# Windowed attention with a sink: the masks move from TensorE products into VectorE's maximum

## The chip, the cores and the metric

The kernel runs on one core of a Trainium2 chip. The metric is the device time of one execution in microseconds (us); a kernel's figure is the median of its timed runs. The core's engines are named as in the profile: PE is TensorE (PEld its weight loads), DVE is VectorE, ACT is ScalarE, POOL is GpSimd and SP is SyncE, which issues most DMAs.

## The reference, cut to what matters

The model is two layers deep, 512 tokens and 256 context tokens wide, with a width of 1024. The first layer ("even") has a gated chunk mixer and a differential attention, the second ("odd") the attention of this change. Each layer ends in a feed-forward of width 2816. The odd attention has 16 query heads of 64 over 4 key heads. A block of 128 queries sees the block before, its own and the next one (within a distance of 128), and all 256 context keys. A learned sink per head enters the softmax as one more score without a value.

```python
mask = ((kpos >= 0)[None, :] & (kpos < s_len)[None, :]
        & (jnp.abs(qpos[:, None] - kpos[None, :]) <= WINDOW))
return sink_attend(qb, [(kb, vb, mask), (kc, vc, None)], sink)
...
def sink_attend(q, kvs, sink):
    ...
        s = jnp.einsum('bqhgd,bkhd->bhgqk', q, k).astype(jnp.float32) * ATTN_SCALE
        if mask is not None:
            s = jnp.where(mask, s, NEG_INF)
    ...
    p = jax.nn.softmax(jnp.concatenate(scores + [s_sink], axis=-1), axis=-1)
```

## The kernel before, in words

Everything is held transposed on chip, features on the 128 partitions, and dense products are made of three products of split operands (a rounded high part and a low part, `mm3`, lines 111 to 117). The stages follow each other: even mixer, feed-forward 0, odd mixer, feed-forward 1. Within a stage the Tile framework's scheduler (`schedule_with_timeline_sim=True`, line 2037) puts the instructions into each engine's queue in an order that it works out from its own timeline; `tc.issue_after` and the helper `run` (lines 46 to 50) tie some of them to a fixed order. Each engine then runs its queue strictly in order. A tile with `bufs=n` has n buffers in turn, and a writer waits until the readers of the old content are done.

Ahead of the odd attention, the keys and values of both kinds of tokens are projected and the keys are rotated and split (`stack`, lines 1740 to 1746). In that stretch the mask is prepared: a DMA brings 128 x 384 values (0 or -1e30) into `mraw`, ScalarE copies its first and last 128 columns into `mask`, copies the identity into `identr`, copies the sink to `sink` and negates `nsink` (lines 1709 to 1715), and takes one exponential so that its table is loaded (line 1716).

`odd` (line 1766) runs `attend(g, half)` for the four key heads g with half 0, then with half 1; each half has two blocks i of 128 queries, so there are 16 row blocks, and `softmax` makes four score tiles (one per query head of the group) in each: 64 tiles. For one tile PE makes the products with the two key parts into a PSUM tile `pw` (lines 1801 to 1803); adds the mask to each neighbour block by a product of the identity and the mask (lines 1804 to 1808); and makes the context products (lines 1809 to 1811). Blocks 0 and 3 have 512 scores a row and one masked neighbour, blocks 1 and 2 have 640 and two, so there are 96 mask products. PSUM tiles of scores come from `wide`, which has two buffers; a buffer holds two tiles of 512 or one of 640.

VectorE then finds the negative row maximum (line 1814) and takes the minimum with the negated sink (line 1815). ScalarE reads the scores from PSUM, adds that value, takes the exponential into the SBUF buffer `e` (7 buffers) and sums the row (line 1817). Four small operations give the reciprocal of the row's sum with the sink (lines 1819 to 1822). PE transposes the exponentials (lines 1839 to 1841), VectorE and ScalarE in turn copy them from PSUM into `pt` (line 1843), and PE multiplies them with the values (lines 1848 to 1853).

PE's other work in this stretch is the projection of later query heads (`project_q`), the output projection of the first half (`project(0, ...)`, line 1911) and the start of that of the second half (lines 1916 to 1927).

Of the kernel before, what the change touches and what calls it, by code (L numbers as in the profile page):

```python
# [7 lines left out]
F32R = mybir.dt.float32r  # L8
BF16 = mybir.dt.bfloat16
I32 = mybir.dt.int32  # L10
AF = mybir.ActivationFunctionType
ALU = mybir.AluOpType
AX = mybir.AxisListType.X

P = 128
# [3 lines left out]
TC = 256  # L19
# [8 lines left out]
class Builder:  # L28
# [17 lines left out]
    def run(self, key, fn, *args, **kw):  # L46

        with self.tc.issue_after(self.tail[key].ins) if key in self.tail else ExitStack():
            self.tail[key] = fn(*args, **kw)  # L49
        return self.tail[key]  # L50
# [1478 lines left out]
    def seam(self, s2_part, Wl, ahead):  # L1529

        tc, nc, a, run = self.tc, self.nc, self.a, self.run
# [5 lines left out]
        X, C = [[[t[:, c] for t in A] for A in self.A] for c in (slice(0, TX), slice(TX, TA))]  # L1537
# [86 lines left out]
        ps = self.fill()  # L1624
# [52 lines left out]
        def products(upto):  # L1677
            for v in order:
                if v == "s":
                    csum.append(self.single())  # L1680
                    sums(csum[0], [sq[1, m] for m in (0, 3, 4, 5, 6, 7)], TC)
                elif v == "d":
                    csum.append(spread(csum[1], self.single()))
                else:
                    (k_x if v[0] == "K" else v_x)(int(v[1]))
                if v == upto:
                    return
# [18 lines left out]
                self.ring, self.ring_cfg = wide  # L1706
        csum.append(diagonal(csum[0], TC))
        products("V7")
        mask = Rk.tile([P, 2, P], F32R, name="mask")
        identr = Rk.tile([P, P], F32R, name="identr")  # L1710
        sink = Rk.tile([P, 16], F32, name="sink2")
        run("ACT", nc.scalar.copy, mask, mraw.rearrange("p (a c) -> p a c", a=3)[:, 0::2, :])
        run("ACT", nc.scalar.copy, identr, self.ident)
        run("ACT", nc.scalar.copy, sink, nsink)
        run("ACT", nc.scalar.mul, nsink, nsink, -1.0)
        run("ACT", nc.scalar.activation, self.small(16), nsink, AF.Exp)
# [3 lines left out]
        qps = [self.fill(), self.single()]  # L1720
        for ps, W2 in zip(qps, Wq):
            for k in range(KT):
                t, c = W2[k // 4], k % 4 * P
# [3 lines left out]
        b = self.bank()  # L1727
# [8 lines left out]
        K = []  # L1736
# [17 lines left out]
        V = []  # L1754
        for tb in range(6):
            v = Rk.tile([P, TC], F32, name=f"v1_{tb}")
# [4 lines left out]
        self.ring, self.ring_cfg = kept  # L1761
        Rt.release()
        self.here = here
        self.kv = qps, X, Rk, tabs, K[0] + K[1], V, mask, identr, sink, nsink

    def odd(self):
        tc, nc, a = self.tc, self.nc, self.a
        qps, X, Rk, tabs, K, V, mask, identr, sink, nsink = self.kv
        Rs = tc.alloc_tile_pool(name="att1", bufs=1, side="right", reuse_waits="tile")
        Qs, scored = {}, {}  # L1770
        stacks = [Rk.tile([P, TX], F32R, name=self.uid(t), tag="sq01", bufs=4) for _ in range(2) for t in ("qa", "qb")]
# [11 lines left out]
        def softmax(g, i, rc):  # L1783


            nm, sums, sk = [self.small(4, "sa", 10) for _ in range(3)]
            b0, b1 = max(0, i - 1), min(4, i + 2)
            w = (b1 - b0) * P
            edge = w + TC <= TX
            st = 0 if edge else TX - w  # L1790
            en = st + w
            es = []
            for x in range(4):
                pair, par = x // 2, x % 2
                if edge:
                    two = self.wide() if par == 0 else two
                    ps = two[:, par * TX:par * TX + TX]
                else:
                    ps = self.wide()
                Q = Qs[2 * g + pair][par][:, i * P:(i + 1) * P]  # L1800
                for p in range(2):
                    nc.tensor.matmul(ps[:, st:en], Q, K[g][p][:, b0 * P:b1 * P], start=p == 0, stop=p == 1,  # L1802
                                     skip_group_check=True)
                for b in range(b0, b1):
                    if b != i:
                        c = st + (b - b0) * P
                        nc.tensor.matmul(ps[:, c:c + P], identr, mask[:, int(b > i), :], start=False, stop=True,
                                         skip_group_check=True)
                for p in range(2):
                    last = nc.tensor.matmul(ps[:, en:en + TC], Q, K[g][p][:, TX:], start=p == 0 and not edge,  # L1810
                                            stop=p == 1, skip_group_check=True)
                scored[g, i, x] = last
                c = nm[:, x:x + 1]
                nc.vector.tensor_reduce(c, ps[:, st:en + TC], axis=AX, op=ALU.max, negate=True)
                nc.vector.tensor_tensor(c, c, nsink[:, 4 * g + x:4 * g + x + 1], ALU.min)
                e = Rs.tile([P, 640], F32, name=self.uid("e"), tag="e1", bufs=7)
                nc.scalar.activation(e[:, :w + TC], ps[:, st:en + TC], AF.Exp, bias=c, accum_out=sums[:, x:x + 1])
                es.append(e)
            nc.vector.tensor_tensor(sk, nm, sink[:, 4 * g:4 * g + 4], ALU.add)
            nc.scalar.activation(sk, sk, AF.Exp)  # L1820
            nc.vector.tensor_tensor(sums, sums, sk, ALU.add)
            nc.vector.reciprocal(rc, sums)
            return es, b0, b1
# [92 lines left out]
        for m in range(2):  # L1916
# [4 lines left out]
            ps = both[:, m * TC:(m + 1) * TC]  # L1921
# [119 lines left out]
```

## Time and profile before

| | |
|---|---|
| median of 3 runs | 1554.86 us (1551.56 to 1555.87) |
| profiled execution | 1551.89 us, span 1550.1 us |
| PE, PEld busy | 1496.6 us (97%), 1344.5 us (87%) |
| DVE, ACT, POOL busy | 1080.4 us (70%), 736.4 us (48%), 816.4 us (53%) |
| granted TensorE clock, mean | 0.997 |

The profile is of one execution. A row of a group names the line of the kernel, the engine, the operation, the tiles it writes and reads, shape and count; then the busy time of the group in us, the mean of one in ns, and the idle time of the engine just before, with what ended it. A row of the timeline begins with start and duration in us; in brackets stands the idle time before it and who ended it. Matmuls are pipelined, so their durations overlap and the distance of starts tells what one costs. "issue" is idle time without a visible cause. A wait for several things is put down to the last of them.

### The profile page before, as it was taken

How to read it: one execution, taken by the hardware profiler on the slowest of the kernel's cores; microseconds unless marked ns; L12 is line 12 of the kernel's file. 1: busy time of each engine (PE TensorE's matmuls, PEld its weight loads, DVE VectorE, ACT ScalarE, POOL GpSimd, SP SyncE). 2: the span in 40 equal slices, each digit the busy share in tenths (PEclk: the TensorE clock that was granted, in tenths of full speed). 3: DMA queues.
4: the chain of work that ended last, by engine and by line, in shares of the span. 5: the costliest groups of instructions: out<-in, count | busy, mean ns of one | idle time of the engine just before them, and what ended most of it. 6: DMA issues, size and time to landing. Idle time of an engine off the chain costs nothing.

```text
span 1550.1 us, 25119 instructions
## 1 busy us (share of the span) xinstructions
PE 1496.6 (97%) x9611; PEld 1344.5 (87%) x9611; DVE 1080.4 (70%) x1922; ACT 736.4 (48%) x1515; POOL 816.4 (53%) x556
## 2 busy tenths in 40 slices
PE   6999899899999999999999998999989999999998
PEld 5758789799989999999999887777869899999997
DVE  6622888765887877888885577665667966666665
ACT  4525566554543333333333345556556544444444
POOL 1353320053077677668776535432314488888882
PEclk9999999999999999999999999999999999999999
DMA  9881100251043243445441312100224232323201
GB/s 352 297 296 51 38 8 1 65 208 41 28 130 116 96 130 116 134 159 170 139 167 52 102 43 68 48 28 21 69 96 164 66 112 90 115 89 116 89 21 55
DMA packets 55464, 162.27 MB, mean 105 GB/s; under 512 B 6192, under 2 KB 8624, under 8 KB 47664
## 3 DMA queue, kind: packets, MB, share of 16 engines
q1 hardware_dynamic: 48288, 135.37, 26.0%
q10 hardware_dynamic: 7056, 25.30, 4.9%
q8 instruction: 75, 1.23, 0.3%
q14 instruction: 45, 0.37, 0.1%
HBM read 158.55 MB, written 2.10 MB: 104 GB/s over the span
## 4 chain that ended last, share of the span: by engine, by line
PE 82%; DVE 13%; ACT 3%; issue 2%; DMA 0%; POOL 0%; DVEq 0%; SPq 0%; ACTq 0%; POOLq 0%
PE pw L116 11%; PE pw L115 11%; PE pw L117 11%; PE pb L115 8%; PE pb L116 8%; PE pb L117 8%; PE pf L115 4%; PE pf L116 4%; PE pf L117 4%; PE pb L1851 2%; PE pb L1840 2%; PE pw L1802 1%; PE pw L1810 1%; PE pf L369 1%; DVE t L49 1%
## 5 line engine op out<-in xcount | busy, mean ns | idle before, releaser
L999 DVE SCALAR_TENSOR_TENSOR xT<-pb,mod,xT 128x512 f32<-128x512 f32 (+3 forms) x204 | 143.2, 709 | 128.7 <-PE pb L117 128.3
L115 PE MATMUL pw<-ax,w 128*128 128x384 f32 (+2 forms) x716 | 226.5, 318 | 3.7 <-DVE q L49 1.9
L116 PE MATMUL pw<-ax,w 128*128 128x384 f32 (+2 forms) x716 | 227.4, 318 | 2.6 <-DVE ax L49 2.4
L117 PE MATMUL pw<-ax,w 128*128 128x384 f32 (+2 forms) x716 | 226.9, 317 | 0.1
L49 POOL TENSOR_TENSOR w<-raw,w 128x512 fp32r<-128x512 f32 x122 | 186.0, 1540 | 48.2 <-ACT w L49 48.1
L92 POOL TENSOR_TENSOR w<-raw,w 128x512 fp32r<-128x512 f32 (+1 forms) x70 | 103.2, 1482 | 161.6 <-ACT w L89 151.4
L49 POOL TENSOR_TENSOR w<-t,w 128x512 fp32r<-128x512 f32 x99 | 147.9, 1498 | 56.3 <-ACT w L49 56.3
L115 PE MATMUL pb<-hh,w 128*128 128x512 f32 x480 | 171.2, 357 | 2.2 <-DVE xT L999 2.2
L117 PE MATMUL pb<-hh,w 128*128 128x512 f32 x480 | 171.7, 358 | 0.4 <-DVE w L49 0.4
L116 PE MATMUL pb<-hh,w 128*128 128x512 f32 x480 | 171.3, 357 | 0.0
L115 PE MATMUL pw<-T,w 128*128 128x384 f32 (+1 forms) x508 | 156.6, 310 | 2.5 <-DVE hs L1207 1.2
L116 PE MATMUL pw<-T,w 128*128 128x384 f32 (+1 forms) x508 | 157.0, 310 | 1.2 <-DVE T L132 1.2
L117 PE MATMUL pw<-T,w 128*128 128x384 f32 (+1 forms) x508 | 157.0, 310 | 0.0
L115 PE MATMUL pf<-ax,w 128*128 128x256 f32 (+2 forms) x460 | 150.5, 327 | 2.9 <-DVE qf L264 1.1
L117 PE MATMUL pf<-ax,w 128*128 128x256 f32 (+2 forms) x460 | 149.5, 325 | 0.0
L116 PE MATMUL pf<-ax,w 128*128 128x256 f32 (+2 forms) x460 | 148.8, 323 | 0.0
L115 PEld LDWEIGHTS pw<-ax,w 128*128 128x128 f32 x716 | 135.5, 190 | 8.5 <-DVE q L49 2.6
L116 PEld LDWEIGHTS pw<-ax,w 128*128 128x128 f32 x716 | 136.0, 190 | 7.8 <-DVE ax L49 3.6
L117 PEld LDWEIGHTS pw<-ax,w 128*128 128x128 f32 x716 | 136.0, 190 | 2.4 <-DVE w L1170 0.4
L49 POOL TENSOR_TENSOR hh<-hs,hh 128x768 fp32r<-128x768 f32 (+1 forms) x42 | 78.0, 1858 | 92.9 <-ACT hh L49 69.1
L49 POOL TENSOR_TENSOR w<-rawo,w 128x512 fp32r<-128x512 f32 x59 | 103.8, 1760 | 29.5 <-ACT w L49 29.5
L240 DVE SCALAR_TENSOR_TENSOR junk<-ar,cb 128x1024 bf16<-128x1024 f32 x64 | 106.8, 1669 | 0.0
(442 smaller groups left out, 3912.0 us busy)
## 6 DMA issues: line engine op xcount, KB each, us to landing
raw<-ffn_in SPq DMA_DIRECT2D x44, 1024.0 KB, 5.3
ar<-ada SPq DMA_DIRECT2D x24, 1024.0 KB, 7.9
ar<-ada ACTq DMA_DIRECT2D x48, 512.0 KB, 3.6
rawo<-ffn_out SPq DMA_DIRECT2D x88, 256.0 KB, 3.0
raw<-odd_out SPq DMA_DIRECT2D x28, 256.0 KB, 2.7
raw<-qk SPq DMA_DIRECT2D x16, 256.0 KB, 7.8
raw<-uv SPq DMA_DIRECT2D x16, 256.0 KB, 3.2
raw<-even_out SPq DMA_DIRECT2D x8, 512.0 KB, 3.5
```

Of the source, the lines that this page charges most:

```text
L49: self.tail[key] = fn(*args, **kw)
L92: eng.tensor_tensor(lo, raw, hi.bitcast(F32), ALU.subtract)
L115: mm(out, s[0], m[0], start=start, stop=False, **kw)
L116: mm(out, s[0], m[1], start=False, stop=False, **kw)
L117: return mm(out, s[1], m[0], start=False, stop=stop, **kw)
L240: return self.nc.vector.scalar_tensor_tensor(junk, t, 1.0, self.cb[who], ALU.mult, ALU.mult, accum_out=self.acc[who][:, col:col + 1])
L369: return run("PE", fn, *args, **kw) if head else fn(*args, **kw)
L999: ins = self.nc.vector.scalar_tensor_tensor(h, ps[:, r], self.modcol(l, j, m, who), h, ALU.mult, ALU.add)
L1802: nc.tensor.matmul(ps[:, st:en], Q, K[g][p][:, b0 * P:b1 * P], start=p == 0, stop=p == 1, skip_group_check=True)
L1810: last = nc.tensor.matmul(ps[:, en:en + TC], Q, K[g][p][:, TX:], start=p == 0 and not edge, stop=p == 1, skip_group_check=True)
L1840: last = nc.tensor.transpose(pt[:, x * P:(x + 1) * P], es[2 * (x % 2) + x // 2][:, kb * P:(kb + 1) * P], self.ident)
L1851: nc.tensor.matmul(po[64 * h:64 * h + 64, :], V[vb][:, 64 * g:64 * g + 64], t[:, h * TC:h * TC + TC], start=kb == 0, stop=kb == nb - 1, sk ...
```

## The change

`mask` becomes a row of six blocks of 128 in bf16: lower neighbour, own, upper neighbour, and three of zeros; GpSimd clears it and ScalarE writes the two neighbour blocks. `identr` and the mask products go. One VectorE instruction per tile adds the tile's stretch of `mask` to the scores, multiplies by -1, writes the result into `e`, and takes the minimum over the row with the negated sink as its first value. The exponential then reads `e` in SBUF, with scale -1 and that minimum as its bias, and writes it in place. Block 3, which has its lower neighbour and own block ahead of the context, reads the row of six in two runs of 256.

```diff
-        mask = Rk.tile([P, 2, P], F32R, name="mask")
-        identr = Rk.tile([P, P], F32R, name="identr")
+        mask = Rk.tile([P, 6, P], BF16, name="mask")
+        nc.gpsimd.memset(mask, 0.0)
         sink = Rk.tile([P, 16], F32, name="sink2")
-        run("ACT", nc.scalar.copy, mask, mraw.rearrange("p (a c) -> p a c", a=3)[:, 0::2, :])
-        run("ACT", nc.scalar.copy, identr, self.ident)
+        run("ACT", nc.scalar.copy, mask[:, 0:3:2, :], mraw.rearrange("p (a c) -> p a c", a=3)[:, 0::2, :])
...
-                for b in range(b0, b1):
-                    if b != i:
-                        c = st + (b - b0) * P
-                        nc.tensor.matmul(ps[:, c:c + P], identr, mask[:, int(b > i), :], start=False, stop=True,
-                                         skip_group_check=True)
                 for p in range(2):
                     last = nc.tensor.matmul(ps[:, en:en + TC], Q, K[g][p][:, TX:], start=p == 0 and not edge,
                                             stop=p == 1, skip_group_check=True)
                 scored[g, i, x] = last
                 c = nm[:, x:x + 1]
-                nc.vector.tensor_reduce(c, ps[:, st:en + TC], axis=AX, op=ALU.max, negate=True)
-                nc.vector.tensor_tensor(c, c, nsink[:, 4 * g + x:4 * g + x + 1], ALU.min)
                 e = Rs.tile([P, 640], F32, name=self.uid("e"), tag="e1", bufs=7)
-                nc.scalar.activation(e[:, :w + TC], ps[:, st:en + TC], AF.Exp, bias=c, accum_out=sums[:, x:x + 1])
+                s, t = ps[:, st:en + TC], e[:, :w + TC]
+                if i == 3:
+                    cut = lambda v: v.rearrange("p (a c) -> p a c", a=2)
+                    s, u, m = cut(s), cut(t), cut(mask.rearrange("p b c -> p (b c)"))[:, :, :TC]
+                else:
+                    u, m = t, mask.rearrange("p b c -> p (b c)")[:, (i == 0) * P:(i == 0) * P + w + TC]
+                nc.vector.tensor_tensor_reduce(u, s, m, -1.0, nsink[:, 4 * g + x:4 * g + x + 1], ALU.add, ALU.min, c)
+                nc.scalar.activation(t, t, AF.Exp, bias=c, scale=-1.0, accum_out=sums[:, x:x + 1])
                 es.append(e)
```

More of the change, by code (lines that the diff above doesn't have):

```diff
@@ L1763, in seam @@
         self.here = here
-        self.kv = qps, X, Rk, tabs, K[0] + K[1], V, mask, identr, sink, nsink
+        self.kv = qps, X, Rk, tabs, K[0] + K[1], V, mask, sink, nsink
     def odd(self):
         tc, nc, a = self.tc, self.nc, self.a
-        qps, X, Rk, tabs, K, V, mask, identr, sink, nsink = self.kv
+        qps, X, Rk, tabs, K, V, mask, sink, nsink = self.kv
         Rs = tc.alloc_tile_pool(name="att1", bufs=1, side="right", reuse_waits="tile")
```

## The prediction, made before the changed kernel was timed

> **What bounds the kernel now.** I read the page first, for the shares of the engines and the chain.
>
> ```profile
> span 1550.1 us, 25119 instructions
> ...
> PE 1496.6 (97%) x9611; PEld 1344.5 (87%) x9611; DVE 1080.4 (70%) x1922; ACT 736.4 (48%) x1515; POOL 816.4 (53%) x556
> ...
> PE 82%; DVE 13%; ACT 3%; issue 2%; DMA 0%; POOL 0%; DVEq 0%; SPq 0%; ACTq 0%; POOLq 0%
> ```
>
> TensorE (PE) is busy nearly all the time and holds 82% of the chain that ended last. That is an average, so the next view is the table of stretches. The first score product of the odd attention starts at 959.83 us and its last transposes end near 1156.8 us; what follows is the projection's end and the second feed-forward.
>
> ```profile
> 959.83:1156.80 196.97, 189.26 (x1322) 147.40 (x1321) 124.20 (x289) 112.59 (x270) 61.44 (x56) 0.99 0.16 53
> 963.00:970.00 7.00, 4.80 (x18) 3.94 (x19) 4.28 (x11) 3.87 (x9) 5.05 (x4) 0.76 0.24 75
> 1157.00:1551.00 394.00, 379.84 (x2679) 355.04 (x2677) 263.93 (x433) 195.12 (x414) 283.95 (x193) 0.99 0.28 91
> ```
>
> The columns after the stretch are its length, then busy time of PE, PEld, DVE, ACT and POOL, then the granted clock and the DMAs. In the 197.0 us of the attention PE lacks only 7.7 us of being always busy. VectorE (DVE) has 72.8 us free and ScalarE (ACT) 84.4. So work taken from PE should show in the time, and VectorE has room for more. After 1157 us PE is busy for 379.84 of 394.00 us and starts from the attention's result, so that part should simply begin earlier by what the attention saves. The waits of PE in the attention say the same:
>
> ```profile
> PE pw L1802 <- ACT e L1817: 3.1, 1, 3.1
> PE pb L1840 <- ACT e L1817: 2.5, 4, 1.5
> PE pf L115 <- DVE qf L264: 1.1, 1, 1.1
> ```
>
> One wait of 3.1 us is for a score bank that ScalarE still reads, and four waits of 2.5 us together are for exponentials to transpose.
>
> **The change, part by part. Mask products.** What one costs can't be read from its duration, since matmuls overlap; it is read from starts.
>
> ```profile
> L1807 PE MATMUL pw<-mask,identr x96: 219/223/307, 960.3 to 1148.4; 128*128 128x128 f32 x96
> ```
> ```profile
> 1023.30 0.28 PE L1802 MATMUL pw<-kl,qb 128*128 128x256 f32 x1
> ...
> 1023.42 0.22 PE L1807 MATMUL pw<-mask,identr 128*128 128x128 f32 x1
> ...
> 1023.48 0.33 PE L1810 MATMUL pw<-kh,qb 128*128 128x256 f32 x1
> ...
> 1023.65 0.28 PE L1810 MATMUL pw<-kl,qb 128*128 128x256 f32 x1
> ...
> 1023.77 0.28 PE L115 MATMUL pf<-ax,w 128*128 128x256 f32 x1
> ```
>
> From the mask's start to that of the second context product are 0.23 us, in which one mask product and one 256-column product run. The 256-column products beside them follow each other at 0.12 us. So a mask costs about 0.115 us: 0.06 for itself and the rest because the next product waits for its weights. 96 of them are 11.0 us, all on PE.
>
> **VectorE: two operations become one.** Now each of the 64 score tiles has a maximum and a small minimum.
>
> ```profile
> L1814 DVE TENSOR_REDUCE sa<-pw 128x1 f32<-128x640 f32 x32 | 26.1, 821 | 5.9 <-PE pw L1810 5.4
> ...
> L1814 DVE TENSOR_REDUCE sa<-pw 128x1 f32<-128x512 f32 x32 | 21.7, 686 | 16.7 <-PE pw L1810 16.4
> L1815 DVE TENSOR_TENSOR sa<-sa,sink 128x1 f32<-128x1 f32 x64 | 15.0, 240 | 1.0
> ```
>
> That is 26.1 + 21.7 + 15.0 = 62.8 us, 0.98 us a tile. The fused operation does not occur in this trace. The nearest rows read a PSUM bank and an SBUF tile and write SBUF; one more prices the reading of an accumulator.
>
> ```profile
> L999 DVE SCALAR_TENSOR_TENSOR xT<-pb,mod,xT 128x512 f32<-128x512 f32 x175 | 129.9, 747 | 122.2 <-PE pb L117 121.9
> ...
> L999 DVE SCALAR_TENSOR_TENSOR xT<-pb,mod,xT 128x256 f32<-128x256 f32 x22 | 10.2, 480 | 2.9 <-PE pb L117 2.9
> ...
> L240 DVE DVE_READ_ACCUMULATOR junk<-ar,cb 128x1 f32 x64 | 5.1, 79 | 0.0
> ```
>
> 256 elements more cost 747 - 480 = 267 ns, so 640 elements are an estimated 747 + 133 = 880 ns. The low end is one pass with nothing more, 32 x (0.747 + 0.880) = 52.1 us; with a separate accumulator read of 79 ns it is 57.2 us. The high end is two passes, the elementwise row plus the reduction's: 0.747 + 0.686 = 1.43 us and 0.880 + 0.821 = 1.70 us, together 100.4 us. I take one pass and the read, 57.2 us: the row of line 999 has the same two kinds of operands and does its arithmetic in one pass. VectorE is then 5.6 us less busy, off PE's path, and worth nothing by itself. The fourth row block's mask is read in two runs of 256; I cost that at zero, since the element count stays 512, and up to some tens of ns could hide in VectorE's free time.
>
> **ScalarE reads SBUF in place of PSUM.**
>
> ```profile
> L89 ACT CAST w<-raw 128x512 fp32r<-128x512 f32 x72 | 44.2, 620 | 55.3 <-PE pw L117 30.0 <-PE pf L117 13.6 <-DMA raw<-odd_out 4.2
> ...
> L1843 ACT COPY pt<-pb 128x512 f32<-128x512 f32 x40 | 23.4, 586 | 19.7 <-PE pb L1840 19.6
> ```
>
> A cast from SBUF takes 620 ns where a copy from PSUM takes 586, so the exponential becomes about 34 ns longer, 2.2 us over 64, beside 84 us that ScalarE has free. It reaches PE only where PE waits for an exponential: at most once in each of 16 row blocks, 0.5 us. [...]
>
> **Banks come free earlier.** Now a score bank is held until the exponential has read it; after the change until VectorE has. Its worth is read from the one long wait, at the start:
>
> ```profile
> 959.42 3.51 DVE L1746 TENSOR_TENSOR kl<-kf,kh 64x256 fp32r<-64x256 f32 x8
> ...
> 962.85 1.28 DVE L1814 TENSOR_REDUCE sa<-pw 128x1 f32<-128x512 f32 x2
> ...
> 964.37 0.69 ACT L1817 ACTIVATE e<-pw,sa 128x512 f32<-128x512 f32 x1 [0.87 <-DVE sa L1815]
> ...
> 965.20 0.38 PE L1802 MATMUL pw<-kh,qb 128*128 128x256 f32 x1 [3.11 <-ACT e L1817]
> ```
>
> VectorE is held by the key split until 962.85, whatever PE does. The first fused operation then ends at 962.85 + 0.75 = 963.60, and PE follows 0.14 us later (as now, 964.37 + 0.69 to 965.20), at 963.74: 1.46 us earlier. The two masks ahead of this wait (0.23 us) save nothing, since the wait swallows them.
>
> **The e buffer is taken earlier.** The fused operation writes e, so it must wait until the transposes of the row block before have read the buffer (7 buffers, 4 tiles a block: the fourth tile reuses the first of the block before). The old maximum did not wait for that. Behind it in VectorE's queue stand copies of transposed tiles (L1843), the row sums and the rope of the next queries; PE's value products wait for those copies. The closest case in the trace is:
>
> ```profile
> 1028.23 0.60 PE L1840 MATMUL pb<-ident,e 128*128 128x128 f32 x4
> ...
> 1028.50 0.69 DVE L1814 TENSOR_REDUCE sa<-pw 128x1 f32<-128x512 f32 x1 [0.79 <-PE pw L1810]
> ```
>
> The transposes end at 1028.83, so the fused operation would start 0.33 us late, and VectorE had idled 0.79 us before anyway. I take zero; the high end is a rival below.
>
> **Setup.** A POOL memset of 768 elements a partition, a cast of the identity less, and ScalarE's mask cast now waits for the memset.
>
> ```profile
> L744 POOL MEMSET kl<- 64x768 f32 x2 | 1.5, 734 | 0.1
> ```
> ```profile
> 928.91 1.29 POOL L265 TENSOR_TENSOR sh<-sh,sin 128x512 f32<-128x512 f32 x1 [6.87 <-DVE sh L263]
> ```
> ```profile
> 929.94 0.37 ACT L1757 COPY v<-pb 128x256 f32<-128x256 f32 x1 [6.88 <-PE pb L117]
> ```
>
> The memset takes some 0.73 us behind the weight splits, and 6.87 us of POOL's idle time follow before the rope. Behind ScalarE's wait stand the small sink operations and the table load, and then 6.88 us of idle time. Cost zero; without that cover, 0.7 us.
>
> **The sum.** 94 masks that the first wait does not swallow are 94 x 0.115 = 10.8 us; the bank wait 1.46; together 12.3. Against it: where PE waits for an exponential, up to one mask a block (16 x 0.115 = 1.8 us) is swallowed in the same way; I take half, 0.9. The longer exponential, 0.5 at most: 0.4. That leaves 11.0 us. The profiled execution took 1551.89 us (1550.1 of span and 1.8 around it), so 1540.9 for one like it. The runs lie between 1551.56 and 1555.87, with the median 1554.86, 3.0 above the profiled one; against the median it is 1543.9.
>
> **The rivals.** *A larger gain, through the clock.* After the first wait the granted clock was 0.76 over 963 to 970, which is 7 x 0.24 = 1.7 us lost; a wait at 1239 did the same.
>
> ```profile
> 1239.32 0.38 PE L115 MATMUL pw<-ax,w 128*128 128x256 f32 x1 [1.90 <-DVE q L49]
> ```
> ```profile
> 1239.60:1243.00 3.40, 3.40 (x15) 3.18 (x15) 3.40 (x5) 0.12 (x1) 3.40 (x3) 0.51 0.21 63
> ```
>
> If the shorter first wait (now 965.20 - 3.11 = 962.09 to 965.20, then 961.86 to 963.74, about 1.9 us) no longer trips it, if the later one is missed too, and no mask is swallowed, the gain is 12.3 + 1.7 + 1.7 + 0.9 = 16.6 and the time 1538.3. Against it: the wait at 1239, no longer than that, did trip it. [...] Chance 0.17.
>
> *No gain: the fused operation makes two passes.* At 1.43 and 1.70 us VectorE is busy 124.2 - 62.8 + 100.4 = 161.8 us, still not the bound, but each tile's maximum comes 0.59 us later. Where nothing covers it, once in each of 16 blocks, 9.4 us of the 11.0 are gone: about 1553. For it: no row of this trace shows the operation. Against it: the one-pass rows. Chance 0.14.
>
> *Slower: VectorE's queue stops at the fourth tile of each block.* If the new order of the work (the scheduler makes it anew) brings that tile ahead of the transposes that free its buffer, all behind it wait, and then PE. At w us in each of 16 blocks the gain is gone at w = 11.0 / 16 = 0.69; at 1.5 us the time is 1554.9 - 11.0 + 24.0 = 1567.9. For it: the margin of 0.33 us above was already negative. Against it: that is the closest of the cases in the trace, and PE still has other products to run. Chance 0.09.
>
> **How the numbers follow.** My forecast, a gain of 5 to 14 us, has 0.60. A measurement of this kernel tells about 0.3% (4.7 us) from no change. So faster is 0.60 + 0.17 = 0.77, within 0.3% 0.14, slower 0.09. The predicted time is the forecast's, 1543.9. The range goes down to 1536 (the larger gain, for a series whose median lies 2 to 3 us lower, as the runs of before allow) and up to 1553, the two-pass case; the slower rival lies outside.
>
> **What would show it.** Right: no rows of line 1807; one VectorE operation a tile at 0.75 to 0.90 us; exponentials of about 0.72 and 0.83 us; score products waiting on VectorE and not on ScalarE; the stretch from the first score product to the last transposes near 186 us, with PE as full as now; the part after it unchanged in length. Wrong: fused operations well over 1 us; PE waits of more than 1 us, many times, for exponentials or for copies behind a held fused operation; a stretch that is as long as now with more idle PE.

## The result and the profile after

The changed kernel takes 1534.40 us (median of 4 runs, 1532.57 to 1534.78); the kernel before, on the same chip, took 1553.21 (4 runs, 1550.97 to 1555.87). The ratio is 0.989, with a 95% interval of 0.9872 to 0.9907: 14 to 20 us less, faster by more than the 0.3% that can be told from no change. The prediction said 1543.9 within 1536 to 1553. The sign was right; the gain, 18.8 us between the medians, is 1.7 times the predicted 11.0, and the time lies 1.6 us below the range. As much of that, 1.65 us, is the kernel before itself: the range was worked out from its earlier median of 1554.86. Beside later runs it had medians of 1551.67 to 1552.00, so the gain is about 17 to 19 us.

The profiled execution took 1534.77 us. Its page:

```profile
span 1533.0 us, 24888 instructions
...
PE 1486.0 (97%) x9515; PEld 1335.0 (87%) x9515; DVE 1077.4 (70%) x1922; ACT 736.7 (48%) x1514; POOL 818.0 (53%) x557
...
PE 84%; DVE 11%; ACT 2%; issue 1%; DMA 0%; DVEq 0%; SPq 0%; ACTq 0%
```

The span is 17.1 us shorter, the busy time of PE only 10.6. The table of stretches shows where the rest is. From here on the stage is counted from the first score product to the end of the transposes of line 1861 (1862 before), the last of the attention. First the kernel before, then the changed kernel with its part after the stage:

```profile
960.06:1156.72 196.66, 188.95 (x1320) 147.13 (x1319) 123.98 (x288) 112.36 (x270) 61.44 (x56) 0.99 0.16 53
```
```profile
960.79:1139.67 178.88, 176.96 (x1224) 135.28 (x1223) 119.81 (x285) 113.28 (x266) 61.24 (x56) 1.00 0.18 60
1139.67:1533.00 393.33, 380.09 (x2681) 355.44 (x2680) 265.53 (x433) 194.67 (x414) 284.11 (x193) 0.99 0.28 90
```

The stage is 17.8 us shorter: PE is busy for 12.0 us less, and its idle time falls from 7.71 us to 1.92, that is by 5.8. The part after the stage is as long as before (393.4 us then). So all of it is in the stage, and a third of it is waits that are gone. The waits of PE in the stage that remain are four kinds, 1.9 us together:

```profile
PE pw L1801 <- DVE sa L1815: 0.9, 3, 0.4
PE pf L115 <- DVE qf L264: 0.4, 1, 0.4
PE pb L1839 <- ACT e L1816: 0.4, 1, 0.4
PE pb L1850 <- DVE pt L1842: 0.2, 1, 0.2
```

The groups of the new instructions, by form:

```profile
L1815 DVE CUSTOM_DVE_ANT_0 e<-pw,mask,sink 128x640 f32<-128x640 f32 x32 | 28.0, 879 | 8.1 <-PE pb L1839 6.4 <-PE pw L1804 1.5
L1816 ACT ACTIVATE e<-e,sa 128x640 f32<-128x640 f32 x32 | 26.6, 830 | 11.5 <-DVE sa L1815 10.8 <-DVE sa L1820 0.5
L1816 ACT ACTIVATE e<-e,sa 128x512 f32<-128x512 f32 x32 | 23.1, 721 | 8.8 <-DVE sa L1815 8.7
L1815 DVE CUSTOM_DVE_ANT_1 e<-pw,mask,sink 128x512 f32<-128x512 f32 x16 | 11.6, 746 | 2.0 <-PE pb L1839 1.0 <-PE pw L1804 0.9
L1815 DVE CUSTOM_DVE_ANT_0 e<-pw,mask,sink 128x512 f32<-128x512 f32 x16 | 11.6, 747 | 1.8 <-PE pb L1839 1.7
...
L1815 DVE DVE_READ_ACCUMULATOR2_ANT sa<- 128x1 f32 x64 | 5.3, 83 | 0.0
```

The fused operation takes 747 and 879 ns and a read of 83 ns, 56.5 us in all, and the mask in two runs (the form with 1 at its end) costs nothing more. Its idle time is telling: before, the maxima stood idle for score products (5.4 and 16.4 us "<-PE pw"); now VectorE waits for the transposes that free an e buffer (6.4 + 1.0 + 1.7), and for scores hardly at all. The scores are there early. A count of PE's order says the same. Take for each of the 16 row blocks how many of the next block's four score tiles stand in PE's queue ahead of the block's first transposes: on average 0.06 before and 1.44 after. The starts in the two traces give the same 0.06 and 1.44, so PE ran its queue in that order. One such place after the change:

```profile
1022.50 0.44 PE L1801 MATMUL pw<-kh,qb 128*128 128x384 f32 x1
...
1023.86 0.44 PE L1801 MATMUL pw<-kh,qa 128*128 128x384 f32 x1
...
1024.56 0.34 PE L1801 MATMUL pw<-kh,qb 128*128 128x384 f32 x1
...
1025.59 0.82 PE L1839 MATMUL pb<-ident,e 128*128 128x128 f32 x6
```
```profile
1022.13 0.73 ACT L1816 ACTIVATE e<-e,sa 128x512 f32<-128x512 f32 x1
```

The three score tiles that begin at 1022.50, 1023.86 and 1024.56 belong to the next block. The last exponential of this block ended at 1022.86, so the transposes at 1025.59 find all they need.

### The profile page after: what moved, and what is told of

It reads as the page before. It is cut to its first block, busy times and chain, and to the rows that moved or that the text cites. A ratio compares the mean times of both kernels' runs of the same rounds, so it can differ in the third digit from the quotient of the medians.

```text
span 1533.0 us, 24888 instructions
## 1 busy us (share of the span) xinstructions
PE 1486.0 (97%) x9515; PEld 1335.0 (87%) x9515; DVE 1077.4 (70%) x1922; ACT 736.7 (48%) x1514; POOL 818.0 (53%) x557
## 4 chain that ended last, share of the span: by engine, by line
PE 84%; DVE 11%; ACT 2%; issue 1%; DMA 0%; DVEq 0%; SPq 0%; ACTq 0%
PE pw L116 11%; PE pw L115 11%; PE pw L117 11%; PE pb L115 9%; PE pb L116 9%; PE pb L117 9%; PE pf L115 4%; PE pf L116 4%; PE pf L117 4%; PE pb L1850 3%; PE pb L1839 2%; PE pw L1801 1%; PE pf L369 1%; DVE t L49 1%; PE pw L1804 1%
## 5 line engine op out<-in xcount | busy, mean ns | idle before, releaser
L49 POOL TENSOR_TENSOR w<-raw,w 128x512 fp32r<-128x512 f32 x122 | 185.5, 1537 | 47.4 <-ACT w L49 47.2
```

## The experiments

The prediction's theory was that PE is the bound of the stage and that what is taken from it shows. The rivals that the result brought up: the banks freed early by VectorE, the shorter chain from scores to exponential, and PE's order, which the scheduler makes anew for every kernel. Kernels e1, e3, e7 and e9 do no masking, and e9 leaves the sink out of the maximum too, so their times are those of less computation. "Ahead" is the count just described; "opening" is the first 25 us of the stage. Times are medians; the runs of the kernel before beside them had medians of 1551.69 (e1 to e4), 1551.67 (e5 to e8) and 1552.00 (e9 to e12). Stage, PE busy and PE idle are those of one profiled execution. PE's busy time is no fixed sum: the same 1224 products are busy for 174.1 us in e3 and 180.3 us in e1, neither with a half clock in the stage, so its differences are good to a few us.

| kernel | mask products | VectorE, per tile | ahead | stage | PE busy | PE idle, opening + rest | time | ratio to before |
|---|---|---|---|---|---|---|---|---|
| before | 96 | maximum, minimum | 0.06 | 196.7 | 188.9 | 4.2 + 3.5 | 1553.2 | |
| changed | 0 | fused | 1.44 | 178.9 | 177.0 | 1.1 + 0.8 | 1534.4 | 0.989 |
| e1 | 0 | maximum, minimum | -0.47 | 194.7 | 180.3 | 3.6 + 10.7 | 1552.5 | 1.0008 |
| e2 | 96 | fused | 1.38 | 186.4 | 186.1 | 0.3 + 0.0 | 1542.4 | 0.9938 |
| e3 | 0 | fused, bank held | 0.75 | 177.8 | 174.1 | 1.5 + 2.2 | 1534.1 | 0.9888 |
| e4 | 0 | fused, minimum | 1.38 | 179.9 | 177.6 | 1.3 + 1.0 | 1535.0 | 0.9893 |
| e5 | 0 | fused | -0.25 | 185.5 | 177.0 | 3.0 + 5.4 | 1539.9 | 0.9929 |
| e6 | 96 | maximum, minimum | 1.06 | 196.8 | 189.5 | 4.6 + 2.7 | 1550.6 | 0.9998 |
| e7 | 0 | maximum, minimum | 0.63 | 190.0 | 181.3 | 3.5 + 5.2 | 1544.6 | 0.9953 |
| e8 | 0 | fused, twice | 0.00 | 203.4 | 186.6 | 3.3 + 13.5 | 1556.0 | 1.0030 |
| e9 | 0 | maximum | 0.94 | 177.8 | 175.5 | 1.5 + 0.8 | 1534.1 | 0.9886 |
| e10 | 192 | maximum, minimum | 0.06 | 206.3 | 200.1 | 2.9 + 3.2 | 1562.4 | 1.0067 |
| e11 | 96 | maximum, minimum, claims e | 0.34 | 195.7 | 188.9 | 3.1 + 3.6 | 1550.5 | 0.9987 |
| e12 | 0 | fused | 1.69 | 180.9 | 177.8 | 2.4 + 0.7 | 1534.7 | 0.9890 |

### e1: the masks out, and nothing else

```diff
-                for b in range(b0, b1):
-                    if b != i:
-                        c = st + (b - b0) * P
-                        nc.tensor.matmul(ps[:, c:c + P], identr, mask[:, int(b > i), :], start=False, stop=True,
-                                         skip_group_check=True)
```

> The kernel before without its 96 mask products; all else, VectorE's maximum and minimum and the exponential from PSUM too, as before. It leaves out the masking. Before, the attention's stretch was 197.0 us with 7.7 us in which PE was not busy; with the change 179.1 and 1.9. Theory A (the masks are worth 11.0 us, and the other 6 us come because VectorE and not ScalarE frees the score banks): 11 to 13 us faster than before, a stretch of 184 to 186 us, 6 to 8 us of it without PE. Rival B (the waits go because the masks go and the order is made anew): 16 to 18 us faster, 179 to 181 us, under 3 us without PE. Rival C (the waits go because the small minimum no longer stands in VectorE's queue): as A here.

Measured: 1552.54 us, ratio 1.0008 (0.9996 to 1.0019). No gain, where A, B and C all had one of 11 us or more. PE is busy for 8.6 us less than before in the stage and idle for 6.6 more; the 2.0 us that remain are lost outside it, where the trace has four stretches at half clock, against one outside the stage before:

```profile
960.54:1155.20 194.66, 180.34 (x1224) 136.19 (x1223) 124.48 (x285) 112.24 (x267) 61.83 (x56) 1.00 0.16 53
```
```profile
PE pb L1835 <- ACT e L1812: 5.1, 6, 1.8
PE pf L115 <- DVE qf L264: 3.7, 2, 2.9
PE pb L1846 <- ACT pt L1838: 2.2, 5, 0.6
```

The time went into waits of transposes for exponentials (5.1 us), of query products for the rope on VectorE (3.7) and of value products for copies (2.2). One of them, on the timelines of PE, VectorE and ScalarE:

```profile
1011.21 0.40 PE L117 MATMUL pf<-ax,w 128*128 128x512 f32 x1
1013.37 0.44 PE L1835 MATMUL pb<-ident,e 128*128 128x128 f32 x2 [1.75 <-ACT e L1812]
```
```profile
1010.50 0.69 DVE L1809 TENSOR_REDUCE sa<-pw 128x1 f32<-128x512 f32 x1
1011.23 1.08 DVE L278 SCALAR_TENSOR_TENSOR qb<-qf,qb 64x512 fp32r<-64x512 f32 x1
1012.34 0.16 DVE L1810 TENSOR_TENSOR sa<-sa,sink 128x1 f32<-128x1 f32 x1
```
```profile
1012.53 0.69 ACT L1812 ACTIVATE e<-pw,sa 128x512 f32<-128x512 f32 x1 [0.27 <-DVE sa L1810]
```

The maximum ends at 1011.19, but an operation of 1.08 us for the queries stands between it and its minimum, which ends at 1012.50. The exponential follows, and PE, which has nothing of the next block ahead of these transposes, waits 1.75 us. So the statement that work taken from PE shows in the time falls, for the masks by themselves.

### e2: the fused operation, with the masks kept on PE

```diff
+                for b in range(b0, b1):
+                    if b != i:
+                        c = st + (b - b0) * P
+                        nc.tensor.matmul(ps[:, c:c + P], identr, mask[:, int(b > i), :], start=False, stop=True,
+                                         skip_group_check=True)
...
-                if i == 3:
-                    cut = lambda v: v.rearrange("p (a c) -> p a c", a=2)
-                    s, u, m = cut(s), cut(t), cut(mask.rearrange("p b c -> p (b c)"))[:, :, :TC]
-                else:
-                    u, m = t, mask.rearrange("p b c -> p (b c)")[:, (i == 0) * P:(i == 0) * P + w + TC]
+                u, m = t, zero[:, 0:1].to_broadcast([P, w + TC])
```

> The changed kernel with the mask products put back on PE; VectorE's fused operation adds a column of zeros in place of the mask. Theory A: 5 to 6 us faster than before, a stretch of 190 to 192 us, about 2 us of it without PE. Rival B: within 1.5 us of before, 7 us without PE. Rival C: as A.

Measured: 1542.35 us, ratio 0.9938 (0.9922 to 0.9955), 9 us less than before with every mask product still there: more than the 5 to 6 us of A and C, and not the nothing of B.

```profile
959.76:1146.14 186.38, 186.09 (x1320) 146.33 (x1319) 118.29 (x285) 113.42 (x266) 61.27 (x56) 1.00 0.17 58
```

PE has 0.29 us of idle time left in 186.4 us. From here the masks' removal is worth 1542.35 - 1534.40 = 8.0 us: in this order, where PE hardly waits, the removal pays.

### e3: the score bank held to the end of the exponential

Not in this diff: the mask row is also multiplied by zero, and the exponential reads the plain scores.

```diff
-                nc.scalar.activation(t, t, AF.Exp, bias=c, scale=-1.0, accum_out=sums[:, x:x + 1])
+                nc.scalar.activation(t, ps[:, st:en + TC], AF.Exp, bias=c, accum_out=sums[:, x:x + 1])
```

> The changed kernel with the exponential reading the scores in PSUM again, so that a bank is held until ScalarE has read it; the fused operation is there as it was, its mask row multiplied by zero. It leaves out the masking. Theory A: 5 to 6 us slower than the changed kernel (11 to 13 faster than before), a stretch of 184 to 186 us, score products waiting on ScalarE again. Rivals B and C: within 1.5 us of the changed kernel, 179 to 180 us.

Measured: 1534.09 us, ratio 0.9888 (0.9872 to 0.9904), as fast as the changed kernel, though PE waits for banks again:

```profile
PE pw L1801 <- ACT e L1816: 2.5, 4, 1.4
```

The early release of the banks is not what the gain comes from, against theory A. e9 below has the whole gain with banks held by ScalarE too.

### e4: a small minimum after the fused operation

```diff
+                nc.vector.tensor_tensor(c, c, nsink[:, 4 * g + x:4 * g + x + 1], ALU.min)
```

> The changed kernel with the small minimum with the sink put back after each fused operation (it changes no value), 64 more VectorE instructions of 0.15 to 0.25 us. Theory A: within 1.5 us of the changed kernel, under 3 us without PE. Rival B: the same. Rival C: 4 to 6 us slower than the changed kernel, PE idle 6 to 8 us.

Measured: 1535.00 us, ratio 0.9893 (0.9877 to 0.9910). Nothing is lost, where C had 4 to 6 us, although the chain is longer. From the end of a tile's last score product to the end of its exponential it takes 4.51 us on average, against 3.35 in the changed kernel, 3.11 before and 3.53 in e1. With 1.38 tiles ahead there is other work for PE meanwhile. So the length of the chain does not decide by itself where scores run ahead.

### e5: an order like that of before forced on the changed kernel

```diff
                 for p in range(2):
-                    nc.tensor.matmul(ps[:, st:en], Q, K[g][p][:, b0 * P:b1 * P], start=p == 0, stop=p == 1,
-                                     skip_group_check=True)
+                    with tc.issue_after(first_tr[-1].ins) if first_tr else ExitStack():
+                        nc.tensor.matmul(ps[:, st:en], Q, K[g][p][:, b0 * P:b1 * P], start=p == 0, stop=p == 1,
+                                         skip_group_check=True)
...
+                    if kb == 0:
+                        first_tr.append(last)
```

> The changed kernel with one tie: PE's score products of a row block come no earlier in its queue than the first transposes of the block before. In PE's queue 1.44 of the next block's four score tiles stood, on average over the 16 blocks, ahead of a block's first transposes; before the change 0.06; with the tie -0.25 (less than zero: a tile of the block itself is still to come). The work of every engine is that of the changed kernel. Theory D (the gain is PE's order: score products further ahead of the transposes leave VectorE and ScalarE time, and only then do the masks' 11 us show): 12 to 17 us slower than the changed kernel, near the kernel before, 10 to 15 us of the stretch without PE. Rival E (the fused operation itself makes the chain from scores to transposes shorter): within 3 us of the changed kernel.

Measured: 1539.93 us, ratio 0.9929 (0.9907 to 0.9951), 5.5 us above the changed kernel, between D (12 to 17) and E (within 3): a little under a third of the gain goes with this order. PE works as long as in the changed kernel (177.0 us, here with 3.4 us at half clock) and waits 6.5 us more, for exponentials above all:

```profile
PE pb L1840 <- ACT e L1817: 2.7, 5, 0.6
PE pw L1802 <- DVE sa L1816: 1.9, 1, 1.9
```

The larger part of the gain stays. e5 and e1 have about the same order by this count (-0.25 and -0.47) and no mask products, yet e5 is 12.6 us faster. From a tile's last score product to the end of its exponential it takes 2.85 us on average, against 3.53 in e1. If PE met that difference of 0.68 us once in each of 16 blocks, it would be an estimated 11 us; so E's shorter chain may hold where no scores run ahead, but no run shows it apart from the rest of the order.

### e6 and e7: the operations of before, with the next block written ahead

In e6 the first three tiles of the next block stand ahead of a block's transposes in the program's text; e7 is e6 without the masks.

```diff
             for x in range(4):
+                if x == 3:
+                    rc = yield
...
+                es, b0, b1 = begun.pop((g, i)).send(rc[:, i % 2 * 4:i % 2 * 4 + 4])
+                if i % 2 == 0:
+                    begin(g, i + 1)
+                elif half and g < 3:
+                    begin(g + 1, 2)
```

> The kernel before with all its operations, masks on PE too; only the order of the program's text differs: the first three score tiles of the next row block (within a head, and from head to head in the second half) are written ahead of a block's transposes. PE's queue then has 1.06 tiles ahead in place of 0.06. Theory D: 7 to 10 us faster than before, under 3 us of the stretch without PE, as where the fused operation ran with the mask products (9.6 us). Rival E: within 2 us of before.

> As the run before it, and without the mask products (it leaves out the masking); VectorE's maximum and minimum and the exponential from PSUM as before the change; 0.63 tiles ahead, where the kernel that merely left out the masks had -0.47. Theory D: 12 to 17 us faster than before. Rival E: within 2 us of before, as the run that merely left out the masks.

Measured: e6 1550.62 us, ratio 0.9998 (0.9988 to 1.0007), no gain, as E said and against D's 7 to 10 us. e7 1544.61 us, ratio 0.9953 (0.9936 to 0.9971), 7 us less, between the two. The first 25 us of e6, beside the same of the changed kernel, show the most of what it loses:

```profile
958.71:983.71 25.00, 20.44 (x98) 17.24 (x96) 16.61 (x32) 12.61 (x28) 12.69 (x10) 0.86 0.22 64
```
```profile
960.50:985.50 25.00, 23.91 (x134) 18.11 (x134) 19.62 (x42) 15.58 (x36) 12.64 (x10) 1.00 0.18 59
```

PE misses 4.6 us there to waits, and the granted clock of 0.86 takes another 3.4. The longest wait is 3.2 us for a score bank, then one of 2.2 us for the rope:

```profile
PE pw L1804 <- ACT e L1819: 3.5, 2, 3.2
PE pf L115 <- DVE qf L264: 2.2, 1, 2.2
```

The rest of the stage gains little either: 171.75 us for 1222 products of PE, against 171.66 for 1214 in the kernel before. So order alone, with the operations of before, gave nothing where the masks stay, though the fused operation gave 9 us there with an order not much further ahead (e2: 1.38, e6: 1.06). Where they are out it let 7 us through, of which e1 had let none.

### e8: the fused operation twice

```diff
+                nc.vector.tensor_tensor_reduce(u, s, m, -1.0, nsink[:, 4 * g + x:4 * g + x + 1], ALU.add, ALU.min, c)
```

> The changed kernel with each fused operation done twice, so that VectorE has 64 more operations of 0.75 to 0.88 us (52 us). PE's queue then has 0.0 tiles ahead. Theory D: near the kernel before or slower (12 to 25 us slower than the changed kernel), since PE's order goes back and VectorE is nearly full. Rival E: 0.83 us more in each of 16 blocks, 10 to 13 us slower than the changed kernel.

Measured: 1556.03 us, ratio 1.0030 (1.0015 to 1.0046), 21.6 us above the changed kernel. D had 12 to 25 us slower, E 10 to 13. VectorE is busy for 164 of 203 us and not the bound, but the second operation costs far more than its 0.83 us once in each of 16 blocks: the scheduler puts no tile ahead any more (0.00), and PE is idle for 16.8 us. Three stretches at half clock, 1.7 us lost in each, fall into the stage as well, whose mean granted clock is 0.97.

```profile
PE pw L1801 <- DVE sa L1816: 7.7, 9, 3.2
```

### e9: masks and minimum out, the rest as before

```diff
-                nc.vector.tensor_tensor(c, c, nsink[:, 4 * g + x:4 * g + x + 1], ALU.min)
```

This is e1 with one line less (the diff leaves out the lines of the mask products, which go here too).

> The kernel before without its mask products and without the small minimum of VectorE: the exponential's bias is the negated maximum itself, so neither the masking nor the sink's part in the maximum is computed. One VectorE operation of 686 or 821 ns then stands between scores and exponential, as after the change, but the exponential still reads PSUM and nothing writes e on VectorE. In the order of PE's queue 0.94 score tiles of the next block stand ahead of a block's first transposes (before 0.06, masks alone out -0.47, changed 1.44). If two operations in a row in place of one are what turned the saved mask products into waits, this stage takes 177 to 182 us, PE idles under 5 us in it, and the time is 14 to 18 us below the kernel before (1534 to 1538). If what matters is that VectorE itself writes e, or its length, it stays with masks-alone-out: stage 190 to 195, PE idle 8 to 14 us, time within 0.3% to 0.6% of before.

Measured: 1534.09 us, ratio 0.9886 (0.9866 to 0.9906), the whole gain without any fused operation.

```profile
961.16:1139.00 177.84, 175.51 (x1224) 135.58 (x1223) 118.04 (x221) 110.73 (x267) 61.73 (x56) 1.00 0.18 60
```
```profile
L1809 DVE TENSOR_REDUCE sa<-pw 128x1 f32<-128x640 f32 x32 | 25.7, 818 | 2.7 <-PE pw L1805 2.7
...
L1809 DVE TENSOR_REDUCE sa<-pw 128x1 f32<-128x512 f32 x32 | 21.5, 684 | 6.1 <-PE pw L1805 5.9
```

The maxima take as long as before and wait for scores 8.6 us in place of 21.8: the scores come early here too, with 0.94 tiles ahead. Between e1 and e9 lie 64 operations of 229 ns on average, on an engine that is 64% busy in the stage, and 18 us. So masks and minimum out are enough for the whole gain, and the rest of the fused operation is not needed for it. It isn't shown that a second operation in VectorE's queue costs this by itself: in e4 one stands there and costs nothing. e1 and e9 also differ in the order that the scheduler made (-0.47 and 0.94).

### e10: the masks twice

```diff
-                        nc.tensor.matmul(ps[:, c:c + P], identr, mask[:, int(b > i), :], start=False, stop=True,
-                                         skip_group_check=True)
+                        for _ in range(2):
+                            nc.tensor.matmul(ps[:, c:c + P], identr, mask[:, int(b > i), :], start=False, stop=True,
+                                             skip_group_check=True)
```

> The kernel before with each of the 96 mask products issued twice (the mask is added twice; minus 2e30 masks as well). The order of score tiles and transposes is as before (0.06). By the prediction's price, 0.06 us for the product and the rest for the wait for its weights (here the same weights and data again), 96 more cost 6 to 11 us and the time is 1557 to 1563 with the stage 202 to 208. If the waits of PE in the kernel before swallow mask products as they swallowed the saving when the masks were taken out, the added ones are swallowed too: within 3 us of before, with PE's idle time in the stage down by as much as its busy time is up.

Measured: 1562.43 us, ratio 1.0067 (1.0050 to 1.0084), 10.4 us above the kernel before, 0.109 us for each of 96 products more. The predicted price of 0.115 holds; the interval of the ratio allows 0.08 to 0.14. The first wait took up the two new products ahead of it, as the prediction had said of the old ones: 3.1 us before, here

```profile
PE pw L1802 <- ACT e L1818: 2.9, 1, 2.9
```

Adding 96 products costs 10.4 us and removing 96 gains nothing (e1). What PE is given lengthens the stage; what is taken from it can turn into waits.

### e11: e claimed on VectorE

```diff
-                nc.vector.tensor_reduce(c, ps[:, st:en + TC], axis=AX, op=ALU.max, negate=True)
-                nc.vector.tensor_tensor(c, c, nsink[:, 4 * g + x:4 * g + x + 1], ALU.min)
                 e = Rs.tile([P, 640], F32, name=self.uid("e"), tag="e1", bufs=7)
+                nc.vector.tensor_reduce(e[:, 0:1], ps[:, st:en + TC], axis=AX, op=ALU.max, negate=True)
+                nc.vector.tensor_tensor(c, e[:, 0:1], nsink[:, 4 * g + x:4 * g + x + 1], ALU.min)
```

> The kernel before with one change: the maximum is written into the first column of e instead of the small tile, and the minimum reads it there. VectorE, PE and ScalarE do the same work, the masks stay on PE, but e is now taken by VectorE, as in the changed kernel, so VectorE waits for the transposes of the block before. If the order that the scheduler makes is better because e is taken there, the time falls by 5 to 10 us as with the fused operation and the masks kept (9.6 us). If the one operation in place of two does it, the time is that of before within 3 us. PE's queue has 0.34 score tiles ahead (before 0.06), which speaks for no change.

Measured: 1550.46 us, ratio 0.9987 (0.9978 to 0.9997), 1.5 us less, and so within the 3 us of no effect. That VectorE takes the e buffer is not what makes the better order.

### e12: the changed kernel with the next block written ahead

The edit of e6, on the changed kernel.

> The changed kernel with the first three tiles of the next block written ahead of the transposes of this one in the program's text, so that the scheduler can run further ahead: 1.69 score tiles of the next block ahead of a block's first transposes, against 1.44. If run-ahead still pays, PE's remaining idle time of 1.9 us in the stage is the most there is to gain: 0 to 2 us below the changed kernel (1532 to 1534.5). If the room is used up, or the e buffers and VectorE's queue now limit, 0 to 3 us above it.

Measured: 1534.70 us, ratio 0.9890 (0.9873 to 0.9908), the time of the changed kernel: running further ahead brings nothing more. Its profiled execution, the slowest of its four at 1536.95, has 3.1 us of idle time in the stage. No kernel of these that does the whole computation beats the changed one.

## Why the prediction was right in its sign and wrong in its size

**The step that failed** is the sentence "So work taken from PE should show in the time", with the waits of PE taken over from the trace of before. The sum was 10.8 for the masks, 1.46 for the first wait, less 1.3 for waits that swallow some of it. It held PE's order fixed, and named a new order only as a way to lose. The stage was to be near 186 us and is 178.9. The runs show two sides of that. The masks alone gain nothing (e1), so the forecast's mechanism by itself was wrong. With the minimum gone from VectorE as well (e9, and the changed kernel), the masks' price comes through and the old waits go too. The 17.8 us of the stage are 12.0 of busy time, of which 1.7 are a half clock that no longer falls in it, and 5.8 of idle time: 2.7 at the first wait, 3.1 elsewhere.

**Mask products.** 0.115 us each, 10.8 or 11.0 in all. e10 gives 0.109. The busy time falls by 12.0 - 1.7 = 10.3 us, which agrees, but is the weaker witness (in e1 it falls by 6.9 without the half clock). The weight loads beside the prediction's example begin 0.12 us apart (at 1023.18, 1023.30, 1023.42 and 1023.53 us in the trace before), the mask's at 1023.30 like the others, though the next product starts 0.06 us after the mask's. The price was right, for products that are added.

**VectorE.** 57.2 us predicted, 56.5 measured; the durations of 0.747 and 0.880 us and the read, from the neighbouring rows, were right. "Worth nothing by itself" was wrong: with every mask kept the fused operation gains 9 us (e2), and leaving out the minimum turns e1's nothing into 18 us (e9), on an engine with time to spare. Whether the minimum's own time does it, its place behind other work in the queue, or the order that the scheduler makes without it, isn't told apart. I had seen the idle time of the maxima (16.4 and 5.4 us "<-PE pw") only as room. It said that for 20 of the 64 tiles VectorE stood ready before the scores were there.

**ScalarE from SBUF.** 721 and 830 ns, against 687 and 795 before: the 34 ns and "about 0.72 and 0.83" were right, and beside 65 us of free ScalarE time PE waited for an exponential once, for 0.4 us.

**The first bank wait.** 1.46 us predicted, 2.7 measured (3.1 to 0.4):

```profile
958.62 3.50 DVE L1745 TENSOR_TENSOR kl<-kf,kh 64x256 fp32r<-64x256 f32 x8
962.15 0.75 DVE L1815 CUSTOM_DVE_ANT_0 e<-pw,mask,sink 128x512 f32<-128x512 f32 x1
```
```profile
962.97 0.39 PE L1801 MATMUL pw<-kh,qb 128*128 128x256 f32 x1 [0.36 <-DVE sa L1815]
```

The fused operation took its 0.75 us and PE followed 0.06 us after the accumulator's read, which the prediction had left out of this term. But the key split ended at 962.12 and not at 962.93, so VectorE began earlier, and PE came later. The prediction had taken VectorE's time there as given "whatever PE does"; it moved with the new order. e3, with a wait of 1.4 us for a bank, is as fast, so the size of this wait mattered little.

**The e buffer.** The wait came, six times:

```profile
DVE e L1815 <- PE pb L1839: 9.1, 6, 2.9
```

9.1 us on VectorE, the longest 2.9, and PE lost at most 0.4 us anywhere. Zero was right, for another reason than the margin of 0.33 us: scores that run ahead of the transposes cause this wait, and by PE's short waits they are also what covers it. The slower rival had its mechanism right and its price wrong.

**The larger gain.** 16.6 us were predicted for it, and about 17 came, but not by its sum. The half clock after the first wait is gone. Elsewhere it returned: in the trace after it begins at 302, 951 and 1183 us, in that of before at 967 and 1240, the last few us of both left aside. With three stretches against two, the clock as a whole gave nothing. The stage began 0.7 us later; the stretch at 951 needn't be the cause, since e2 and e3 have one at 949 and begin at 959.76 and 959.56. In its trace e5 ran for 3.4 us at half clock right after a wait of 1.90 us, while a wait of 2.9 us at the same place in e1 was followed by none:

```profile
959.09:962.50 3.41, 1.51 (x10) 1.02 (x9) 3.31 (x10) 3.04 (x8) 0.86 (x1) 1.00 0.25 77
```
```profile
962.50:965.90 3.40, 3.40 (x11) 2.81 (x12) 2.46 (x6) 2.19 (x6) 3.32 (x4) 0.50 0.39 120
```
```profile
960.37:963.79 3.42, 1.98 (x13) 1.45 (x11) 3.38 (x8) 2.22 (x5) 1.68 (x2) 1.00 0.09 34
963.79:967.20 3.41, 1.93 (x8) 1.61 (x9) 2.02 (x4) 0.78 (x2) 3.33 (x3) 1.00 0.50 154
```

So the length of one wait does not tell it, as the prediction had found of the wait at 1239. Where a wait falls does go with it in the traces. Away from the end of a trace each stretch at half clock lasts 3.413 us in the clock's record of the traces before and after, and in all 14 traces these stretches begin whole multiples of that after the clock first became full: before at 966.57 and 1239.64 us, 278 and 358 times 3.413 after 17.67; after the change at 302.10, 950.64 and 1182.74 us, 84, 274 and 342 times after 15.38. Cut into such intervals, e5's wait lies in one of them (the first row, PE idle for 1.90 us), and so does the wait at 1239 (1.90 us in 1236.23 to 1239.64); e1's is split over two (the last rows, 1.44 and 1.48 us). In the 14 traces each of the 26 intervals with more than 1.88 us of idle PE was followed by half clock (five of them before and after the change: 2.04, 1.90 and 2.30 us, then 2.15 and 3.41); of the 65 with 1.24 to 1.88 us, 18 were (two of eight before and after). Why is not shown.

**Two passes.** They didn't come. 9.4 us were predicted for a maximum 0.59 us later; e8, with one 0.83 to 0.96 us later (an estimated 13 to 15 us by the same working), lost 21.6. The same failure of the same step: another operation changes the order, not only the waits.

**Setup and the tail.** The memset took 748 ns at 891 us; ScalarE waited for it once, for 0.7 us, well ahead of the stage. The part after the stage kept its 393.3 us. Right.

**What stays open.** What is shown is that the masks' removal alone gains nothing (e1), the fused operation alone 9 us (e2), and masks and minimum out the whole (e9). PE's order carries a part of the gain: 5.5 us by e5, about 8 by e7 against e1, none by e6. How much of the rest is the shorter chain (e5 against e1) isn't told apart, nor why the scheduler makes the better order. Taking the minimum out brings it (e9), but putting one behind the fused operation does not take it away (e4). Claiming e does not bring it (e11), and a longer operation takes it away (e8). Each of these kernels is one order, so its last few us may be that order's luck. Nor does the count of tiles ahead tell all: e6 has 1.06 and gains nothing. The opening alone, with an order fixed by hand, wasn't tried.

## What to carry to other kernels

With PE 97% busy, 96 added products cost their full 10.4 us here, but 96 removed ones gained nothing by themselves: ask first what PE would wait for next, and whether each consumer has work queued ahead of it. A sign of too little is idle time of the consumer "<-PE" tile after tile, such as the 21.8 us of the maxima here, for 20 of 64 tiles. It is a sign and no measure: e7 still has 20.6 us of it and is 7 us faster. Where a scheduler makes the order, two small operations that stand in a row in the text need not stand in a row in the queue, and removing one can be worth more than its duration; try each part of a change alone and both together, since the parts here gave 0 and 9 us, and together 17 or more.

## What was not expected of the hardware

The small operations of 128 x 4 on VectorE took 371 and 324 ns on average (lines 1820 and 1818) after the change, but 214 and 163 in e4, and 412 and 282 in e9. The means hide two kinds:

```profile
L1820 DVE TENSOR_TENSOR sa<-sa,sa x16: 148/162/1235, 974.3 to 1129.7; 128x4 f32<-128x4 f32 x16
```
```profile
L1818 DVE TENSOR_TENSOR sa<-sa,sink x16: 150/164/1302, 971.4 to 1128.8; 128x4 f32<-128x4 f32 x16
```

The middle number is the median: most take about 163 ns, and a few up to 1.3 us. The longest of line 1818, beside GpSimd's timeline:

```profile
1085.02 1.30 DVE L1818 TENSOR_TENSOR sa<-sa,sink 128x4 f32<-128x4 f32 x1
```
```profile
1085.01 1.29 POOL L92 TENSOR_TENSOR w<-raw,w 128x512 fp32r<-128x512 f32 x1 [3.52 <-ACT w L89]
```

GpSimd's operation began just before it, and VectorE's ended with it. So it is with all the long ones: between 900 and 1200 us of the 14 traces VectorE has 896 such operations, which read two small tiles in SBUF. 160 take more than 250 ns (10 of 96 before, 8 of 32 after the change), and each of these ends 11 to 26 ns after an operation of GpSimd (13 to 19 before, 19 to 25 after). The minimum of line 1815 is of this kind (median 159 ns, mean 240): some 5 of its 15.0 us, estimated as 64 times the 81 ns between, lie in the long ones. The fused operation, which reads PSUM and one tile in SBUF, shows none: its 64 took 739 to 752 ns at 512 elements and 867 to 884 at 640. That this is why the minimum's removal pays is not shown: e4's small operations lose 8.1 us in this way, those of the kernel before 5.5, and e4 is as fast as the changed kernel.
